# Row factors of four norms from a spread sum: inverse root on ScalarE and one Newton step, beside re-pinned copies and transposes

## Chip, cores and metric

The kernel runs on one core of a Trainium2 chip. The metric is the device time in microseconds of one execution. PE is TensorE, DVE is VectorE, ACT is ScalarE, POOL is GpSimd, SP is SyncE (which issues most DMAs). PSUM is the memory that matmuls write to, SBUF the one that the other engines work in.

## The reference

One layer of a hybrid encoder, S = 512 tokens, D = 2048 channels, float32:

```python
xn   = rms_norm(x, attn_norm_g)                    # norm 1, over 2048 channels
proj = xn @ w_in                                   # u_val, u_gate, q, k, v: 1024 columns each
h    = u_val * sigmoid(u_gate)                     # group A
h    = depthwise_conv(h, 31 taps) + dw_b
y_a  = silu(layer_norm(h, ln_g, ln_b))             # norm "ln", over 1024 channels
y_b  = neighborhood_attention(q, k, v, rpb)        # group B: 16 heads of 64, window 8 x 16 on an 8 x 64 grid
mixed = concat(rms_norm(y_a, conv_out_g), rms_norm(y_b, na_out_g))   # norms "a" and "na"
x    = x + mixed @ w_out
up   = depthwise_conv(rms_norm(x, ffn_norm_g) @ w_up, 3 taps) + b    # norm 2; 2 x 5632 columns
x    = x + (silu(gate) * val) @ w_down
out  = rms_norm(x, final_norm_g)                   # norm 3
```

Each norm needs, for every token, one over the root of (mean square + 1e-6).

## The kernel before

Activations lie with channels on the 128 partitions and tokens along the free axis, so a factor per token has to be known on all partitions: a tile of 128x512 whose rows are all alike. Products are made in parts: every float32 operand is split in a high and a low float32r tile, and one product becomes three matmuls (`mm3`, L124 to L129: high by high L127, high by low L128, low by high L129). The weights arrive in units of 128x1024 (`raw`, DMA by SP); `parts` (L113 to L118) has ACT copy the high half (`whi`, L116) and DVE subtract the low one (`wlo`, L117). Three units are prepared ahead of the one that PE reads, in four buffers.

The order of the work is written out: units follow a plan, and the first stage projects group A's columns (`a`), the values (`v`) and queries and keys (`q`) in the order "aavaav", four times "aq", "qqqq". After each weight unit `tick` advances two lists of generators, `steps` (norms, attention) and `asteps` (group A's tail), so that pieces of other work are placed between the products. `pin` (`tc.keep_in_program_order`) holds an instruction at its place in its engine's program order; the rest is ordered by a scheduler. Each engine executes its own queue in order.

The norms. `sum_sq` (L165 to L170) adds up squares over the 128-row pieces in a tile `acc`: ACT squares, DVE adds. What is left is a sum over partitions. `rsqrt_steps` (L179 to L214) makes it by one matmul of each 128 columns of `acc` with a column of ones (L190; 128x1, four of them for 512 tokens, each shown as two records in the trace), so that tokens lie on partitions; DVE and ACT make the root on 128x4 numbers (`root`, L172 to L177: Sqrt on ACT, reciprocal and a Newton step on DVE); DVE writes the factors into a diagonal matrix `dg`, high and low (L197, L201); two matmuls of ones with `dg` (L207) put them on all partitions, and ACT copies the result from PSUM (L213). It serves `rstd1` (norm 1), `rln` (ln), `ra` (a), `rna` (na), `rstd2` (norm 2) and `rstd3` (norm 3).

The places that the change touches:

- The start (L220 to L264): ACT makes `xh` with the gains `g1`, which DVE copies out of the first load (L263).
- `project_v` (L310 to L338): the first half's products (`pv`, L324 to L326) end in four PSUM banks. ACT copies each, scaled by the tokens' factor, to `vg` (L335) and `vx` (L338). Three of the banks are the three that `project` cycles through.
- `group_a` (L389 to L418): the mean (`yh`, `yl`, `st` L396, `mu` L398), differences (L401), the factor `rln`, then y·rln (L410), the swish, the splits `ma`, the sums of squares and the factor `ra`.
- The attention turns table and scores by 128x128 transposes on PE (`trp`, L503), 16 for a group.
- `norm_b` (L590) makes `rna`, `stats2` (L662 to L671) makes `rstd2` from two sums that come back by DMA.
- The tail (L991 to L1059). Tokens 0 to 383 are finished with channels on partitions: `finish` (L975 to L989) multiplies by gain and factor, for pairs 0, 2, 3, 5 and 6 on DVE (`fin`, L985, factor `st` read in PSUM), for pairs 1, 4 and 7 on POOL (L983, factor `rb`, a copy in SBUF that ACT makes at L1015). The last 128 tokens are turned and multiplied meanwhile (`pt`, L1028 to L1035); their own factor comes from row sums by ACT (L1038), a root (L1047 to L1051), and the results leave as `out_N` (L1059) behind the `out_T` of `finish`, all on SP's queue.

Of the kernel before, what the change touches and what calls it, by code (L numbers as in the profile page):

```python
# [16 lines left out]
P = 128  # L17
# [49 lines left out]
def layer(ctx: ExitStack, tc: tile.TileContext, xT, xG, xw, w_a, w_in, w_v, w_out, w_up, w_down, par, tab, g3, out, last_out):  # L67
# [23 lines left out]

    pin = tc.keep_in_program_order

    g1 = consts.tile([P, KD], F32, name="g1")
# [18 lines left out]
    def parts(raw, n):  # L113
        hi = wpool.tile([P, U * P], F32R, tag="whi", name="whi", bufs=NW)
        lo = wpool.tile([P, U * P], F32R, tag="wlo", name="wlo", bufs=NW)
        i = nc.scalar.activation(hi[:, :n], raw[:, :n], AF.Copy)  # L116
        j = nc.vector.tensor_sub(lo[:, :n], raw[:, :n], hi[:, :n].bitcast(F32))  # L117
        return hi, lo, i, j  # L118
# [5 lines left out]
    def mm3(ps, w, wk, mh, ml, start, stop):  # L124
        hi, lo = w[:2]
        a = slice(wk * P, (wk + 1) * P)
        nc.tensor.matmul(ps, hi[:, a], mh, start=start, stop=False)  # L127
        nc.tensor.matmul(ps, hi[:, a], ml, start=False, stop=False)  # L128
        return nc.tensor.matmul(ps, lo[:, a], mh, start=False, stop=stop)  # L129


    steps, asteps = [], []
# [31 lines left out]
    def sum_sq(acc, src, first, to=slice(0, S)):  # L164
        if first:  # L165
            nc.scalar.activation(acc, src, AF.Square)
        else:
            q = t2("sq")[:, to]
            nc.scalar.activation(q, src, AF.Square)
            nc.vector.tensor_add(acc, acc, q)  # L170

    def root(r, y, v):  # L172
# [6 lines left out]
    def rsqrt_steps(acc, n, name, to=slice(0, S), keep=True, by_token=None, free=False, rest=1, hold=False):  # L179

        def bank():
            if free:
                return psa.tile([P, 2, S], F32, tag="sc", name="st")[:, 0]
            return psa.tile([P, S], F32, tag="po", name="st")

        m = (to.stop - to.start) // P
        ps = bank()[:, :m]
        v, r, y = (sm.tile([P, S // P], F32, tag="rs" + c, name="rs" + c)[:, :m] for c in "vry")
        for i in range(m):
            nc.tensor.matmul(ps[:, i:i + 1], acc[:, to.start + i * P:to.start + (i + 1) * P], ones[:, 0:1],  # L190
                             start=True, stop=True)
        nc.vector.tensor_scalar(v, ps, 1.0 / n, EPS, op0=ALU.mult, op1=ALU.add)
        root(r, y, v)
        if by_token is not None:
            by_token.append(y)
        ds = [t2("dg", F32R)[:, :m * P] for _ in range(2)]
# [6 lines left out]
        for _ in range(rest):  # L203
            yield
        ps = bank()[:, :m * P]
        for i, dg in enumerate(ds):
            m = nc.tensor.matmul(ps, ones_r, dg, start=i == 0, stop=i == 1)  # L207
            if hold:
                pin(m)
        if not keep:  # L210
            return ps
        res = t2(name)
        nc.scalar.activation(res, ps, AF.Copy)  # L213
        return res  # L214
# [18 lines left out]
    for k in range(KD):  # L233
# [28 lines left out]
        if k == 0:  # L262
            pin(nc.vector.tensor_copy(g1, raw[:, n - KD:n]))  # L263
    with tc.issue_after(last.ins):  # L264
# [18 lines left out]
    def stats1():  # L283
        yield
        for k in range(CH, KD):
            with tc.issue_after(made[0][3].ins):
                sum_sq(acc1, x1[k], False)
            if k % 4 == 3:
                yield
        for _ in range(STAT_AT):  # L290
            yield
        rstd.append((yield from rsqrt_steps(acc1, D, "rstd1", by_token=rtok)))

    steps.append(stats1())

    def project(n):
        ps = psm.tile([P, S], F32, tag="mm", name="pj")
        for u in range(KD // U):
            w = weights()
            for k in range(U):  # L300
                kk = u * U + k
                m = mm3(ps, w, k, xs[kk][0], xs[kk][1], kk == 0, kk == KD - 1)
            tick(m)
            while late and rstd:
                late.pop(0)()
        return ps
# [3 lines left out]
    def project_v(half):  # L310
# [22 lines left out]
        with shifted(-600):  # L333
            for t, ps in enumerate(banks):
                nc.scalar.activation(vg[half][t], ps, AF.Copy, scale=y[:, t:t + 1])  # L335
                for x, rows in ((t - 1, slice(0, DH)), (t, slice(DH, P))):
                    if 0 <= x < len(vx[half]):
                        nc.scalar.activation(vx[half][x][rows], ps[rows], AF.Copy, scale=y[rows, t:t + 1])  # L338

# [49 lines left out]
    def group_a():  # L389
        h, l = t2("yh", F32R), t2("yl", F32R)  # L390
        nc.scalar.activation(h, ysum[0], AF.Copy)
        nc.vector.tensor_sub(l, ysum[0], h.bitcast(F32))
        yield
        ps = psa.tile([P, S], F32, tag="po", name="st")
# [5 lines left out]
        for i in range(NC_):  # L400
            nc.vector.tensor_sub(ys[i], ys[i], mu)  # L401
# [93 lines left out]
    def turn(ts):  # L495
        pts, first = {}, True
        for n in (2, 3, 0, 1):
# [31 lines left out]
    def attention():  # L529
# [18 lines left out]
        values(*before)  # L548
        yield

# [39 lines left out]
    def norm_b():  # L590
        r = yield from rsqrt_steps(acc_na, NA, "rna")
        for i in range(NP_):
# [69 lines left out]
    def stats2():  # L662
# [5 lines left out]
        nc.vector.tensor_add(acc2, acc2, q)  # L668
# [323 lines left out]
    for d in range(KD):  # L992
        ps = psm.tile([P, S], F32, tag="mm", name="pd")[:, fm]
        for k in range(n):
            mm3(ps, ws[d // CH * CH + k], d % CH, hs[k][0][:, fm], hs[k][1][:, fm], k == 0, k == n - 1)
        nc.vector.tensor_add(x2[d][:, fm], x2[d][:, fm], ps)
# [4 lines left out]
    stats, rb, xg = rsqrt_steps(acc, D, "rstd3", to=fm, keep=False, hold=True), [], []  # L1001
# [4 lines left out]
    def spread(g, k):  # L1006
        if (g, k) == (0, 1):
            next(stats)
        elif (g, k) == (1, 2):
            try:  # L1010
                next(stats)
            except StopIteration as e:
                rb.append(e.value)
            rb.append(t2("rb")[:, fm])
            nc.scalar.activation(rb[1], rb[0], AF.Copy)  # L1015
        for at in pairs[:2 if rb else 0]:
            pairs.remove(at)
            finish(at, rb[at % 3 == 1], at % 3 == 1, at % 3 != 1)

    for g, ps in enumerate(banks):  # L1020
# [5 lines left out]
        for k in range(n):  # L1026
            (hh, hl), (dh, dl) = hs[k], ws[g * CH + k]
            i = nc.tensor.matmul(ps, hh[:, tm], dh, start=False, stop=False)  # L1028
            if (g, k) == (1, 2):
                pin(i)  # L1030
                spread(g, k)
            i = nc.tensor.matmul(ps, hl[:, tm], dh, start=False, stop=False)
            if (g, k) == (1, 2):
                pin(i)
            nc.tensor.matmul(ps, hh[:, tm], dl, start=False, stop=k == n - 1)  # L1035
            if (g, k) != (1, 2):
                spread(g, k)
        nc.scalar.activation(t2("sq"), ps, AF.Square, accum_out=sums[:, g:g + 1])  # L1038
# [10 lines left out]
    nc.vector.reciprocal(r, r)  # L1049
    nc.vector.scalar_tensor_tensor(y, r, w, r, op0=ALU.mult, op1=ALU.mult)  # L1050
# [86 lines left out]
```

## Time and profile before

| | us |
|---|---|
| median of three runs | 2025.43 (2024.95, 2025.43, 2026.96) |
| profiled execution, its own time | 2026.78 |
| its span in the profile | 2025.0 |
| PE busy | 2013.7 (99%) |
| DVE busy | 1668.0 (82%) |
| ACT busy | 1052.0 (52%) |
| POOL busy | 168.7 (8%) |

The profile shows one execution. In a line of its timeline stand the start, the duration, the engine, the line of the kernel, the operation, what it writes and reads, the shapes and, with x, how many stand together; in brackets the idle time of the engine just before it and what ended it. A line of the waits names the waiting group, what it waited for, and the sum, count and largest wait. A line of the windows gives length, busy time and count for PE, PEld (TensorE's loading of weights), DVE, ACT and POOL, the clock granted to TensorE (1 is full), the share of the DMA engines and the GB/s that they moved. Matmuls overlap in PE's pipeline, so the distance between two starts, not the duration, is what one costs.

### The profile page before, as it was taken

How to read it: one execution, taken by the hardware profiler on the slowest of the kernel's cores; microseconds unless marked ns; L12 is line 12 of the kernel's file. 1: busy time of each engine (PE TensorE's matmuls, PEld its weight loads, DVE VectorE, ACT ScalarE, POOL GpSimd, SP SyncE). 2: the span in 40 equal slices, each digit the busy share in tenths (PEclk: the TensorE clock that was granted, in tenths of full speed). 3: DMA queues.
4: the chain of work that ended last, by engine and by line, in shares of the span. 5: the costliest groups of instructions: out<-in, count | busy, mean ns of one | idle time of the engine just before them, and what ended most of it. 6: DMA issues, size and time to landing. Idle time of an engine off the chain costs nothing.

```text
span 2025.0 us, 28150 instructions
## 1 busy us (share of the span) xinstructions
PE 2013.7 (99%) x10556; PEld 1721.0 (85%) x10556; DVE 1668.0 (82%) x2300; ACT 1052.0 (52%) x1686; POOL 168.7 (8%) x199
## 2 busy tenths in 40 slices
PE   9999999999999999999999999999999999999998
PEld 8788888888888998888888888888888888888887
DVE  7976888988577899888888888888888888879875
ACT  6323344466346555555555555555555555555563
POOL 0000000000001101111111111111111111110111
PEclk9999999999999999999999999999999999999999
DMA  7223333336338765565565565565565565564573
GB/s 257 94 85 93 113 94 106 106 112 231 104 119 214 198 167 146 125 146 146 125 146 146 129 142 146 127 143 146 118 153 146 125 146 146 125 144 127 146 201 132
DMA packets 98935, 284.25 MB, mean 140 GB/s; under 512 B 10992, under 2 KB 12272, under 8 KB 98800
## 3 DMA queue, kind: packets, MB, share of 16 engines
q1 hardware_dynamic: 72144, 231.07, 36.8%
q0 software_dynamic: 26656, 51.39, 16.9%
q8 instruction: 83, 1.36, 0.3%
q14 instruction: 52, 0.43, 0.1%
HBM read 227.89 MB, written 54.53 MB: 139 GB/s over the span
## 4 chain that ended last, share of the span: by engine, by line
PE 98%; DVE 1%; ACT 0%; issue 0%; DMA 0%; ACTq 0%; DVEq 0%
PE pu L759 27%; PE pu L765 14%; PE pd L129 8%; PE pd L127 8%; PE pd L128 8%; PE pj L127 6%; PE pj L129 5%; PE pj L128 5%; PE po L127 3%; PE po L129 3%; PE po L128 3%; PE pv L325 1%; PE pv L324 1%; PE pv L326 1%; PE trp L503 1%; PE pu L127 1%
## 5 line engine op out<-in xcount | busy, mean ns | idle before, releaser
L116 ACT ACTIVATE whi<-raw 128x1024 fp32r<-128x1024 f32 x364 | 384.6, 1058 | 507.8 <-PE pj L128 137.9
L117 DVE TENSOR_TENSOR wlo<-raw,whi 128x1024 fp32r<-128x1024 f32 x364 | 444.4, 1222 | 210.1 <-ACT whi L116 203.3
L759 PE MATMUL pu<-xc,whi 128*128 128x512 f32 x2352 | 580.0, 391 | 0.0
L759 PEld LDWEIGHTS pu<-xc,whi 128*128 128x128 f32 x2352 | 433.5, 188 | 83.0
L765 PEld LDWEIGHTS pu<-xc,wlo 128*128 128x128 f32 x2352 | 306.9, 191 | 14.7
L765 PE MATMUL pu<-xc,wlo 128*128 128x256 f32 x2352 | 311.4, 282 | 0.0
L129 PE MATMUL pd<-hh,wlo 128*128 128x512 f32 x640 | 250.3, 391 | 0.0
L127 PE MATMUL pd<-hh,whi 128*128 128x512 f32 x640 | 249.7, 390 | 0.0
L128 PE MATMUL pd<-hl,whi 128*128 128x512 f32 x640 | 249.1, 389 | 0.0
L913 POOL DMA_DIRECT2D x2d<-pdc x160 | 139.4, 873 | 1097.8 <-ACT pdc L912 870.9
L127 PE MATMUL pj<-xh,whi 128*128 128x512 f32 x512 | 199.6, 394 | 2.3 <-ACT vx L338 2.2
L129 PE MATMUL pj<-xh,wlo 128*128 128x512 f32 x512 | 199.2, 392 | 0.0
L128 PE MATMUL pj<-xl,whi 128*128 128x512 f32 x512 | 198.9, 391 | 0.0
L791 ACT ACTIVATE pl<-pu 128x256 f32<-128x256 f32 x294 | 109.8, 382 | 149.9 <-PE pu L759 142.8
L379 DVE SCALAR_TENSOR_TENSOR y<-ch,prm,y 128x500 f32<-128x500 f32 (+14 forms) x240 | 173.5, 740 | 4.3
L116 ACT ACTIVATE whi<-ws 128x1024 fp32r<-128x1024 f32 x132 | 139.7, 1058 | 70.9 <-PE pu L759 55.2
L117 DVE TENSOR_TENSOR wlo<-ws,whi 128x1024 fp32r<-128x1024 f32 x132 | 161.1, 1221 | 14.8 <-ACT whi L116 14.8
L129 PEld LDWEIGHTS pd<-hh,wlo 128*128 128x128 f32 x640 | 120.1, 188 | 28.5 <-DVE wlo L117 3.3
L128 PEld LDWEIGHTS pd<-hl,whi 128*128 128x128 f32 x640 | 120.2, 188 | 24.9 <-DVE hl L898 0.3
L127 PEld LDWEIGHTS pd<-hh,whi 128*128 128x128 f32 x640 | 120.4, 188 | 22.6
L912 ACT ACTIVATE pdc<-pd 128x512 f32<-128x512 f32 x160 | 93.8, 588 | 79.3 <-PE pd L129 66.2
L127 PEld LDWEIGHTS pj<-xh,whi 128*128 128x128 f32 x512 | 96.6, 189 | 23.5 <-ACT vx L338 2.6
(220 smaller groups left out, 2728.9 us busy)
## 6 DMA issues: line engine op xcount, KB each, us to landing
raw<-in_w_up SPq DMA_DIRECT2D x176, 512.0 KB, 3.8
raw<-in_w_down SPq DMA_DIRECT2D x88, 512.0 KB, 4.0
x2d<-pdc POOLq DMA_DIRECT2D x160, 256.0 KB, 4.9
raw<-in_w_in SPq DMA_DIRECT2D x60, 512.0 KB, 3.8
raw<-in_w_out SPq DMA_DIRECT2D x32, 512.0 KB, 3.7
raw<-in_w_v SPq DMA_DIRECT2D x16, 512.0 KB, 3.7
tab<-in_tab SPq DMA_DIRECT2D x32, 256.0 KB, 5.1
x<-in_xT SPq DMA_DIRECT2D x16, 256.0 KB, 5.4
```

Source lines behind the costliest of these rows:

```text
L116: i = nc.scalar.activation(hi[:, :n], raw[:, :n], AF.Copy)
L117: j = nc.vector.tensor_sub(lo[:, :n], raw[:, :n], hi[:, :n].bitcast(F32))
L127: nc.tensor.matmul(ps, hi[:, a], mh, start=start, stop=False)
L128: nc.tensor.matmul(ps, hi[:, a], ml, start=False, stop=False)
L129: return nc.tensor.matmul(ps, lo[:, a], mh, start=False, stop=stop)
L324: nc.tensor.matmul(ps, xh, wh[:, f], start=kk == 0, stop=False)
L379: nc.vector.scalar_tensor_tensor(y[:, a:b], h[:, a + j - PAD:b + j - PAD], prm[:, o + j:o + j + 1], y[:, a:b], op0=ALU.mult, op1=ALU.add)
L759: i = nc.tensor.matmul(ps, w[0][:, k * P:(k + 1) * P], comb[c][k], start=k == 0, stop=stop and k == ks[-1])
L765: i = nc.tensor.matmul(ps[:, H:], w[1][:, k * P:(k + 1) * P], comb[c][k][:, :H], start=False, stop=stop and k == U - 1)
L791: nc.scalar.activation(to, ps, AF.Copy)
L912: nc.scalar.activation(t, ps, AF.Copy)
L913: nc.gpsimd.dma_start(xd[d], t, accum_op=ALU.add)
```

## The change

It has six parts.

- Four norms (`rln`, `ra`, `rna`, `rstd2`) and `rstd3` no longer sum into columns. In the new `spread`, ACT copies `acc` to a high part `nh` and DVE makes the low part `nl`; two matmuls with a 128x128 matrix of ones put the sum over the partitions on every partition at once; ACT applies the inverse root straight to PSUM (scale 1/n, bias eps), and three DVE instructions of full width make a Newton step. `factor` wraps it. `rstd1` keeps the old way (`factor_and_tokens`), since its factors are needed by token too; its root uses the same inverse root instead of Sqrt and reciprocal.
- `project_v` pins its copies in order, and the next `whi` copy is pinned behind them (`copied`).
- The first product behind a group of transposes is pinned (`turned`).
- `tick` can advance `asteps` once in the middle of a unit; `group_a`'s mean uses it. The numbers of steps between parts of the norms are set anew.
- The copy of `g1` at the start moves from DVE to ACT.
- In the tail one `rstd` in SBUF serves DVE and POOL, the products with `nh` and `nl` stand at another place of the loop, a dummy inverse root on ACT stands in the middle of the last channel loop, and the last tokens' root is an inverse root, without the reciprocal.

```diff
@@ parts
         i = nc.scalar.activation(hi[:, :n], raw[:, :n], AF.Copy)
+        if copied:
+            copied.pop()
+            pin(i)
@@ mm3
-        nc.tensor.matmul(ps, hi[:, a], mh, start=start, stop=False)
+        m = nc.tensor.matmul(ps, hi[:, a], mh, start=start, stop=False)
+        if turned:
+            turned.pop()
+            pin(m)
@@ tick
-    def tick(behind):
+    def tick(behind, mid=False):
         for todo in (steps, asteps):
-            while todo:
+            while todo and mid == (todo is asteps and amid[0]):
                 try:
                     with tc.issue_after(behind.ins):
-                        next(todo[0])
+                        at = next(todo[0])
+                    if todo is asteps:
+                        amid[0] = at == "mid"
                     break
@@ root
-        nc.scalar.activation(r, v, AF.Sqrt)
-        nc.vector.reciprocal(r, r)
+        nc.scalar.activation(r, v, AF.Abs_reciprocal_sqrt)
@@ in place of rsqrt_steps (whose old body stays for rstd1 as factor_and_tokens)
+    def spread(acc, to, n, name, bank, hold=False):
+        m = to.stop - to.start
+        h, l = (t2("n" + c, F32R)[:, :m] for c in "hl")
+        nc.scalar.activation(h, acc[:, to], AF.Copy)
+        nc.vector.tensor_sub(l, acc[:, to], h.bitcast(F32))
+        yield
+        ps = bank()[:, :m]
+        for i, x in enumerate((h, l)):
+            x = nc.tensor.matmul(ps, ones_r, x, start=i == 0, stop=i == 1)
+            if hold:
+                pin(x)
+        r, q = t2(name)[:, :m], t2("q")[:, :m]
+        nc.scalar.activation(r, ps, AF.Abs_reciprocal_sqrt, scale=1.0 / n, bias=eps)
+        nc.vector.scalar_tensor_tensor(q, r, -0.5 / n, r, op0=ALU.mult, op1=ALU.mult)
+        nc.vector.scalar_tensor_tensor(q, ps, n * EPS, q, op0=ALU.add, op1=ALU.mult)
+        nc.vector.scalar_tensor_tensor(r, q, 1.5, r, op0=ALU.add, op1=ALU.mult)
+        return r
...
+    def factor(acc, n, name, rest=1, free=False):
+        steps = spread(acc, slice(0, S), n, name, lambda: stat_bank(free))
+        next(steps)
+        for _ in range(rest):
+            yield
...
@@ the start
-            pin(nc.vector.tensor_copy(g1, raw[:, n - KD:n]))
+            pin(nc.scalar.activation(g1, raw[:, n - KD:n], AF.Copy))
@@ project
                 m = mm3(ps, w, k, xs[kk][0], xs[kk][1], kk == 0, kk == KD - 1)
+                if k == U // 2:
+                    tick(m, mid=True)
@@ project_v
-                nc.scalar.activation(vg[half][t], ps, AF.Copy, scale=y[:, t:t + 1])
+                pin(nc.scalar.activation(vg[half][t], ps, AF.Copy, scale=y[:, t:t + 1]))
...
-                        nc.scalar.activation(vx[half][x][rows], ps[rows], AF.Copy, scale=y[rows, t:t + 1])
+                        pin(nc.scalar.activation(vx[half][x][rows], ps[rows], AF.Copy, scale=y[rows, t:t + 1]))
+        copied.append(half)
@@ group_a
-        yield
+        yield "mid"
...
-        yield
-        yield
-        r = yield from rsqrt_steps(acc, CONV, "rln")
+        r = yield from factor(acc, CONV, "rln", rest=3)
+        yield
...
-        yield
-        yield
-        ra.append((yield from rsqrt_steps(acc, CONV, "ra")))
+        ra.append((yield from factor(acc, CONV, "ra", rest=2)))
@@ attention
+        turned.append(pts)
         return pts
...
         values(*before)
-        yield
@@ norm_b, stats2
-        r = yield from rsqrt_steps(acc_na, NA, "rna")
+        r = yield from factor(acc_na, NA, "rna")
...
-        yield
-        yield
-        rstd2.append((yield from rsqrt_steps(acc2, D, "rstd2", free=True, rest=5, hold=True)))
+        rstd2.append((yield from factor(acc2, D, "rstd2", rest=2, free=True)))
@@ the tail
+        if d == KD // 2:
+            with tc.issue_after(i.ins):
+                pin(nc.scalar.activation(idle, eps, AF.Abs_reciprocal_sqrt))
...
+    rows = spread(acc, fm, D, "rstd3", stat_bank, hold=True)
+    next(rows)
...
-            rb.append(t2("rb")[:, fm])
-            nc.scalar.activation(rb[1], rb[0], AF.Copy)
...
-            finish(at, rb[at % 3 == 1], at % 3 == 1, at % 3 != 1)
+            finish(at, rb[0], at % 3 == 1, at % 3 != 1)
...
-    nc.scalar.activation(r, v, AF.Sqrt)
+    nc.scalar.activation(r, v, AF.Abs_reciprocal_sqrt)
     nc.vector.tensor_scalar(w, v, -0.5, None, op0=ALU.mult)
-    nc.vector.reciprocal(r, r)
```

More of the change, by code (lines that the diff above doesn't have):

```diff
@@ new lines, in stat_bank, with factor_and_tokens @@
+    def stat_bank(free=False):
+        if free:
+            return psa.tile([P, 2, S], F32, tag="sc", name="st")[:, 0]
+        return psa.tile([P, S], F32, tag="po", name="st")
+    def factor(acc, n, name, rest=1, free=False):
[3 more added lines that the diff above has]
+            yield
+        try:
+            next(steps)
+        except StopIteration as e:
+            return e.value
+    def factor_and_tokens(acc, n, name, by_token):
+        m = S // P
+        ps = stat_bank()[:, :m]
+        v, r, y = (sm.tile([P, m], F32, tag="rs" + c, name="rs" + c) for c in "vry")
@@ L189, in rsqrt_steps @@
         for i in range(m):
-            nc.tensor.matmul(ps[:, i:i + 1], acc[:, to.start + i * P:to.start + (i + 1) * P], ones[:, 0:1],
-                             start=True, stop=True)
+            nc.tensor.matmul(ps[:, i:i + 1], acc[:, i * P:(i + 1) * P], ones[:, 0:1], start=True, stop=True)
         nc.vector.tensor_scalar(v, ps, 1.0 / n, EPS, op0=ALU.mult, op1=ALU.add)
         root(r, y, v)
-        if by_token is not None:
-            by_token.append(y)
-        ds = [t2("dg", F32R)[:, :m * P] for _ in range(2)]
+        by_token.append(y)
@@ L197, in rsqrt_steps @@
+        ds = [t2("dg", F32R) for _ in range(2)]
         nc.vector.tensor_mul(ds[0].rearrange("p (i k) -> p i k", k=P), ident.unsqueeze(1).broadcast_to([P, m, P]),
@@ L202, in rsqrt_steps @@
                                            op0=ALU.mult, op1=ALU.subtract)
-        for _ in range(rest):
-            yield
-        ps = bank()[:, :m * P]
+        yield
+        ps = stat_bank()
         for i, dg in enumerate(ds):
[L207 to L211, printed above, removed]
+            nc.tensor.matmul(ps, ones_r, dg, start=i == 0, stop=i == 1)
         res = t2(name)
@@ L291, in stats1 @@
             yield
-        rstd.append((yield from rsqrt_steps(acc1, D, "rstd1", by_token=rtok)))
+        rstd.append((yield from factor_and_tokens(acc1, D, "rstd1", rtok)))
     steps.append(stats1())
```

34 lines of the change are left out of this document (14 added, 20 removed).

## The prediction

> **What bounds the kernel now.** I read the page first: span, engines, chain.
>
> ```profile
> span 2025.0 us, 28150 instructions
> PE 2013.7 (99%) x10556; PEld 1721.0 (85%) x10556; DVE 1668.0 (82%) x2300; ACT 1052.0 (52%) x1686; POOL 168.7 (8%) x199
> PE 98%; DVE 1%; ACT 0%; issue 0%; DMA 0%; ACTq 0%; DVEq 0%
> ```
>
> TensorE (PE) is busy 2013.7 of 2025.0 us and carries 98% of the chain that ended last, so a microsecond counts if PE loses or saves it, or if it lies in the tail behind the last product. DVE (82%) costs nothing by itself, except where PE waits for its result. Then I read the waits of PE for the longest one, and the timeline and the windows around it:
>
> ```profile
> PE pj L127 <- ACT vx L338: 2.2, 1, 2.2
> 94.15 0.39 PE L326 MATMUL pv<-wlo,xh 128*128 128x512 f32 x1
> 94.35 1.06 ACT L116 ACTIVATE whi<-raw 128x1024 fp32r<-128x1024 f32 x1 [4.38 <-PE pv L325]
> 95.32 0.67 ACT L335 ACTIVATE vg<-pv,rsy 128x512 f32<-128x512 f32 x1
> 96.00 0.68 ACT L338 ACTIVATE vx<-pv,rsy 64x512 f32<-64x512 f32 x1
> 96.73 0.50 PE L127 MATMUL pj<-xh,whi 128*128 128x512 f32 x1 [2.19 <-ACT vx L338]
> 97.70:101.20 3.50, 3.50 (x10) 2.69 (x10) 3.39 (x6) 3.44 (x6) 0.00 (x0) 0.51 0.49 145
> ```
>
> After the first value projection PE needs the first of three banks back. ACT has idled 4.38 us, then makes a whi of a later unit before it copies vg and vx out of that bank, and PE stands. The last line (length; busy PE, PEld, DVE, ACT, POOL with counts; granted clock; DMA share; GB/s) has PE at half clock for 3.5 us right behind it. These are the only microseconds which PE loses in one piece.
>
> **The change, part by part.** All sums are first against the profiled execution: 2026.78 us, of which the span is 2025.0. The median of the three runs shown is 2025.43, 1.35 lower.
>
> *A, the bank's release.* The pins put that whi behind the copies. Bank 0's last product starts nine steps of 0.23 (rows in B) before 94.15, at 92.1, and ends at 92.5, so vg and vx (0.67 + 0.68) are done about 93.9, before PE is there at 94.38. The stall of 96.73 − 94.38 = 2.35 (94.38 is the step after 94.15) goes. The whi, moved to the end of the copies at about 99.4, belongs to a unit that PE reads about 110; that hides it, and without that cover it would cost its own 1.06. The half clock cost 3.50 × (1 − 0.51) = 1.71. Gone with its cause: A = −2.35 − 1.71 = −4.06. Whether every execution loses that clock, one trace can't say; against the median I credit half, so +0.85 there. By the Trainium skill (page "TensorE: Matmul & The Clock Gate", section "What's actually happening") the clock falls only after an idle window of about 3.4 us; the trace disagrees, 2.35 us of rest stand ahead of the 0.51. By that rule A would be −2.35 and the sum 1.71 higher.
>
> *B, the sums over columns.* Four norms lose eight 128x1 products each; the two products with dg become two with nh and nl, at no cost.
>
> ```profile
> L190 PE MATMUL st<-ones,acc x38: 164/250/271, 41.5 to 2006.1; 128*128 128x1 f32 x38
> 433.39 0.39 PE L129 MATMUL pj<-xh,wlo 128*128 128x512 f32 x1
> 434.90 0.49 PE L127 MATMUL pj<-xh,whi 128*128 128x512 f32 x1
> 561.16 0.39 PE L129 MATMUL po<-mah,wlo 128*128 128x512 f32 x1
> 561.39 0.95 PE L190 MATMUL st<-ones,accna 128*128 128x1 f32 x8
> 562.20 0.49 PE L127 MATMUL po<-mah,whi 128*128 128x512 f32 x1
> 562.52 0.40 PE L128 MATMUL po<-mal,whi 128*128 128x512 f32 x1
> 562.75 0.40 PE L129 MATMUL po<-mah,wlo 128*128 128x512 f32 x1
> ```
>
> At the na norm the product before the columns starts at 561.16, the third behind them at 562.75: 1.59, where three steps of 0.23 (562.52 to 562.75) take 0.69. So eight columns cost 0.90. At rln the gap is 434.90 − 433.39 = 1.51 against 562.20 − 561.16 = 1.04, so 0.90 + 0.47 = 1.37 (a wait for acc is in it). The first row (38 alike, rstd1's eight stay) lets me take 0.90 for ra and 0.90 for rstd2. B = −4.07. On the other engines, a diagonal on DVE becomes one copy on ACT, one subtraction and three 512-wide steps on DVE, 0.6 to 0.7 each; they cost where PE waits (E, F).
>
> *C, transposes.* Six groups split 12 + 4 become 16 in a row.
>
> ```profile
> 442.73 0.40 PE L129 MATMUL pj<-xh,wlo 128*128 128x512 f32 x1
> 443.03 0.66 PE L503 MATMUL trp<-ident,tab 128*128 128x128 f32 x4
> 443.44 0.48 PE L127 MATMUL pj<-xh,whi 128*128 128x512 f32 x1
> 443.76 0.39 PE L128 MATMUL pj<-xl,whi 128*128 128x512 f32 x1
> ```
>
> Entering takes 0.30 and the product after leaving 0.32 where 0.23 is the step: 0.07 + 0.09, about 0.14 with rounding. C = 6 × 0.14 = −0.84, between 0 and −1.
>
> *D, the start.* ACT makes the g1 copy it now waits for.
>
> ```profile
> 5.79 0.72 ACT L251 ACTIVATE xh<-raw,g 128x512 fp32r<-128x512 f32 x1 [1.31 <-DVE g L263]
> ```
>
> At most the 1.31 goes, at least nothing, if another input is late next; I take −0.3.
>
> *E, ra's norm.* In the changed kernel's order on PE the two products with nh and nl stand right behind twelve transposes, some 6 us of PE work earlier than the pair they replace. PE is in order; whatever is late there stops everything queued behind, the last ma products and four transposes first.
>
> ```profile
> 413.74 0.69 DVE L398 TENSOR_SCALAR mu<-st 128x512 f32<-128x512 f32 x1 [2.95 <-PE st L396]
> 414.35 1.22 DVE L117 TENSOR_TENSOR wlo<-raw,whi 128x1024 fp32r<-128x1024 f32 x1
> 415.48 2.49 DVE L401 TENSOR_TENSOR y<-y,mu 128x512 f32<-128x512 f32 x4
> 444.85 1.90 DVE L410 TENSOR_TENSOR y<-y,rln 128x512 f32<-128x512 f32 x3 [2.07 <-ACT rln L213]
> 473.81 1.47 PE L503 MATMUL trp<-ident,tab 128*128 128x128 f32 x12
> 477.28 0.69 DVE L170 TENSOR_TENSOR acc<-acc,sq 128x512 f32<-128x512 f32 x1
> ```
>
> The sum for mu is moved four products up, so mu starts at 413.74 − 0.91 = 412.83. Between mu and the first y·rln DVE has 37 instructions at 0.60 (2.49 for four) and four wlo at 1.13 (414.35 to 415.48), with hops some 27.4: y·rln at about 440.3, 4.5 earlier. From there to the end of the last acc takes, as before, 477.97 − 444.85 = 33.1: 473.4. A wlo stands ahead of nl (1.13), then nl 0.69: 475.2. PE is there at 473.81 − 1.37 − 0.14 + 1.23 (twelve transposes) + 0.23 = 473.8. So a new PE wait of 1.4 us; bounds 0 and 4 (ACT's and DVE's order may slip by two wlo). Half a clock window behind it, up to 1.71, stays in the range.
>
> *F, rstd2.* No eight columns, but nh and nl, with another engine step between, now follow an add that a DMA releases:
>
> ```profile
> 683.66 0.69 DVE L668 TENSOR_TENSOR acc<-acc,sq 128x512 f32<-128x512 f32 x1 [0.57 <-DMA sq<-sq]
> ```
>
> nh ends about 685.0 and nl about 686.1; PE comes to them about 686.0 and 686.2. I take +0.2, between 0 and 1.5.
>
> Without the tail: −4.06 − 4.07 − 0.84 − 0.3 + 1.4 + 0.2 = −7.67.
>
> *G, the tail.*
>
> ```profile
> 2005.13 0.40 PE L1032 MATMUL pt<-dh,hl 128*128 128x512 f32 x1
> 2006.22 0.48 PE L1035 MATMUL pt<-dl,hh 128*128 128x512 f32 x1
> 2010.41 5.90 POOL L983 TENSOR_TENSOR fin<-x,rb 128x384 f32<-128x384 f32 x6 [37.65 <-ACT rb L1015]
> 2010.36 3.24 DVE L985 SCALAR_TENSOR_TENSOR fin<-x,prm,st 128x384 f32<-128x384 f32 x6 [0.47 <-ACT rb L1015]
> 2014.12 2.18 DVE L985 SCALAR_TENSOR_TENSOR fin<-x,prm,st 128x384 f32<-128x384 f32 x4
> 2015.44 2.50 SPq L987 DMA_DIRECT2D out_T<-fin  x4
> 2018.55 0.16 DVE L1049 RECIPROCAL rsr<-rsr 128x1 f32<-128x1 f32 x1
> 2019.71 1.82 SPq L1059 DMA_DIRECT2D out_N<-xg  x4
> ```
>
> The columns of rstd3 go (2006.22 − 2005.13 − 0.23 = 0.86) and the reciprocal (0.2): −1.1 if nothing else changes. But DVE's ten fin take their factor from st in PSUM today, while POOL's six take it from the copy rb in SBUF; they run side by side at 0.54 and 0.98 us. In the changed kernel both read x and one rstd in SBUF, at the same time, from about 2010.0. No row of before has DVE with two SBUF inputs beside POOL, so the cost lies between 0 and full turn-taking. If DVE's ten go first (5.4), POOL ends its fourth at 2010.0 + 5.4 + 3.9 = 2019.3; SP sends in order: that pair 0.45, four more 2.3 (2.50 now), the last pair 0.45, four out_N 1.82: 2024.3, against 2021.53 today, so about +2.7 for the tail. If they alternate, DVE's ten end near 2021.1 (5.4 + 5.9 later), and the second half of xg and the root behind them come 4.2 late. The Trainium skill speaks against this change here (page "SBUF — State Buffer", section "Who interferes with whom"): a DVE instruction with two SBUF inputs and a GpSimd instruction that reads SBUF exclude each other for a whole instruction; no run shown bears it out. I take +2.7, which lies between the bounds 0 − 1.1 and +4.2.
>
> Sum: −7.67 + 2.7 = −5.0: 2021.8 in the profiled execution's terms, 2025.43 − 5.0 + 0.85 = **2021.3** as a median.
>
> **The rivals.**
>
> No contention at the end: the two engines go on at 0.54 and 0.98. For it speaks that they overlap without loss today; against it, that DVE's second input moves from PSUM to where POOL reads. −7.67 − 1.1 = −8.8, so 2017.5.
>
> The new wait at ra is two to three us longer than I count, because ACT or DVE works off more of its queue ahead of nh and nl; 82% of DVE busy speaks for it. About 2024.
>
> It doesn't do what it says: something else still keeps the banks after project_v (say, the copies are released later than I read), the 2.35 and the clock remain: 2021.3 + 2.35 + 0.85 = 2024.5.
>
> Slower: the chain of group A on DVE doesn't move, because what set 444.85 was not the mean but the list between. Then the last acc ends at 477.97, nl about 479.8, and PE, waiting from 473.8, loses 6.0 instead of 1.4: +4.6, and two half-clock windows of 1.71 as behind the stall at 97 us: +3.4. 2021.3 + 8.0 = 2029.3. It gets slower than before once PE's wait at that place, clock included, exceeds my 1.4 by over 4.1.
>
> **How the numbers follow.** Tail contention as forecast 0.46 (own range 2020 to 2023.5: from half of it to alternating); no contention 0.26; the longer wait 0.11; no effect on the bank 0.06; slower 0.11. The range 2016.6 to 2024.6 takes the first four in, with about one microsecond below the no-contention sum for the clock that I credited half; it leaves out the slow case and the edges, under 2 in 10. A difference under 0.2% (4.05 us) can hardly be told from none here. Faster by over that is under 2021.38: all of no contention and half of the forecast, 0.49. Slower by over that is above 2029.48: half of the slow case, whose 2029.3 stands at that edge, 0.06. The rest, 0.45, is the same.
>
> **What the profile after would show.** A: no wait of PE on vx, granted clock 1.0 at 95 to 101 us, that whi behind nine copies. B: no 128x1 products but rstd1's. C: groups of 16 transposes. E: a PE wait on nl of 1 to 2 us behind twelve transposes near 470; none makes me wrong by 1.4, over 5 means the slow rival. G: mean durations of fin: if DVE's stay near 0.54 and POOL's near 0.98, I am wrong by 3.8 and the no-contention rival holds; if POOL's last fin ends some 5 us later than today relative to the last product, I am right. A loss spread evenly over PE's products, with the same waits, would make the whole way of counting wrong.

## The result: slower, not faster

The changed kernel takes 2031.95 us (median of nine runs, 2030.62 to 2032.47), the kernel before 2026.67 in the same nine rounds: a ratio of 1.0029, 95% interval [1.0019, 1.0038]. The forecast was 2021.3, with 2024.6 as the upper end. In the profiled executions it is 2031.56 against 2026.78, +4.78 us.

The kernel before has two levels, and its medians lie on one or the other by chance: 24 runs of one later comparison stand at 2024.92 to 2025.88 (11) and at 2026.63 to 2027.77 (13), about 1.6 apart. The traced execution, one of the upper level, has the half clock behind the stall on vx; run 6, without that stall, has one level alone.

The head of the page, the chain and the waits of PE, after:

```profile
span 2029.8 us, 28055 instructions
PE 2008.3 (99%) x10518; PEld 1715.8 (85%) x10518; DVE 1672.3 (82%) x2269; ACT 1052.8 (52%) x1688; POOL 170.5 (8%) x199
PE 97%; DVE 1%; ACT 1%; DMA 0%; issue 0%; ACTq 0%; DVEq 0%
PE trp L537 <- ACT pt L542: 6.2, 6, 1.1
PE po L131 <- DVE oa L637: 2.4, 2, 2.0
```

PE is busy for 5.4 us less than before, and yet the span is 4.8 longer. The wait on vx is gone; six waits of 0.85 to 1.07 on a copy of a turned tile (`pt`, in six of the eight groups; two groups stay split) and two on `oa` have come. To see how much each place is worth, I take the same instruction in both traces and subtract its starts; what the difference changes by between two such marks was won or lost there:

| mark (before, after) | difference | change, and what lies in the stretch |
|---|---|---|
| first product of pv (50.86, 51.22) | +0.36 | +0.36, the start |
| last product of pv (184.86, 181.10) | −3.76 | −4.12, project_v |
| last value product of the attention (555.61, 556.45) | +0.84 | +4.60, rln, ra and the transposes |
| first product with mbh (584.58, 587.47) | +2.89 | +2.05, rna |
| last product pu (1947.71, 1949.62) | +1.91 | −0.98, rstd2 |
| end of the span (2025.0, 2029.8) | +4.8 | +2.9, the tail |

**project_v.** ACT's timeline and the window of the half clock, after:

```profile
92.90 0.69 ACT L371 ACTIVATE vg<-pv,rsy 128x512 f32<-128x512 f32 x1 [2.56 <-PE pv L362]
93.60 0.68 ACT L374 ACTIVATE vx<-pv,rsy 64x512 f32<-64x512 f32 x1
...
99.41 2.00 ACT L117 ACTIVATE whi<-raw 128x1024 fp32r<-128x1024 f32 x2
97.70:101.20 3.50, 3.50 (x17) 2.92 (x16) 3.36 (x6) 3.49 (x5) 0.00 (x0) 1.00 0.00 0
```

vg starts at 92.90 instead of 95.32, the whi follows at 99.41, and the clock is 1.00 with 17 products where 10 had fitted.

**The transposes.** The timeline around the first group, before and then after:

```profile
258.11 1.48 PE L503 MATMUL trp<-ident,tab 128*128 128x128 f32 x12
259.04 1.56 ACT L508 ACTIVATE pt<-trp 128x512 f32<-128x512 f32 x3
260.65 0.66 PE L503 MATMUL trp<-ident,tab 128*128 128x128 f32 x4
```

```profile
254.34 1.47 PE L537 MATMUL trp<-ident,tab 128*128 128x128 f32 x12
255.27 1.55 ACT L542 ACTIVATE pt<-trp 128x512 f32<-128x512 f32 x3
256.88 0.66 PE L537 MATMUL trp<-ident,tab 128*128 128x128 f32 x4 [1.07 <-ACT pt L542]
```

In both, the thirteenth transpose starts right after ACT's third copy (260.60 and 256.82). Before, five products filled the time between (from 259.34; the expectation of run 1 says six). The pin took them away, and PE stands.

**The na norm.** Rows of DVE, and the product that waits, after:

```profile
560.06 0.69 DVE L637 TENSOR_TENSOR oa<-po,ra 128x512 f32<-128x512 f32 x1
565.29 0.69 DVE L205 SCALAR_TENSOR_TENSOR q<-rna 128x512 f32<-128x512 f32 x1 [0.78 <-ACT rna L204]
567.47 1.90 DVE L627 TENSOR_TENSOR ao<-ao,rna 128x512 f32<-128x512 f32 x3
575.00 0.69 DVE L637 TENSOR_TENSOR oa<-po,ra 128x512 f32<-128x512 f32 x1
575.75 0.50 PE L131 MATMUL po<-mah,whi 128*128 128x512 f32 x1 [1.99 <-DVE oa L637]
```

Between two oa, each of which frees a bank of PSUM, DVE has the Newton step (565.29 to 567.47) and the products and splits of the norm. Before, the next oa came at 566.56 and 577.52, eleven microseconds apart; here it is fifteen.

**The tail.** The fin, and SP's last output, after:

```profile
2011.80 9.91 DVE L1017 SCALAR_TENSOR_TENSOR fin<-x,prm,rstd 128x384 f32<-128x384 f32 x10
2011.91 7.80 POOL L1015 TENSOR_TENSOR fin<-x,rstd 128x384 f32<-128x384 f32 x6 [37.23 <-DVE rstd L207]
2021.63 0.68 DVE L1077 TENSOR_TENSOR xg<-pt,g3b 128x512 f32<-128x512 f32 x1
2022.16 0.41 SPq L1021 DMA_DIRECT2D out_T<-fin  x1
2024.56 1.80 SPq L1091 DMA_DIRECT2D out_N<-xg  x4
```

Ten fin on DVE take 9.91 instead of 5.4, six on POOL 7.80 instead of 5.90, and xg, which leads to the last tokens' root, stands behind them. SP has issued the last out_T at 2022.57 and then waits for that root until 2024.56; meanwhile the DMA engines run nearly empty. The groups of fin by line (shortest, median and longest duration in ns), and a window of that pause:

```profile
L1017 DVE SCALAR_TENSOR_TENSOR fin<-x,prm,rstd x10: 605/1350/1374, 2011.8 to 2021.1; 128x384 f32<-128x384 f32 x10
L1015 POOL TENSOR_TENSOR fin<-x,rstd x6: 1308/1321/1385, 2011.9 to 2018.4; 128x384 f32<-128x384 f32 x6
2024.20:2025.20 1.00, 0.00 (x0) 0.00 (x0) 0.99 (x2) 1.00 (x2) 0.00 (x0) 0.50 0.17 65
```

The two engines take turns. While POOL works, DVE's fin start 1.27 to 1.30 us apart (2012.34, 2013.63, 2014.93 and so on), one to each fin of POOL; the three that start after POOL has ended are 0.53 apart.

### The profile page after: what moved, and what is told of

The parts are those of the page before. It is cut to its first block, busy times and chain, and to the rows that moved or that the text cites. A ratio compares the mean times of both kernels' runs of the same rounds, so it can differ in the third digit from the quotient of the medians.

```text
span 2029.8 us, 28055 instructions
## 1 busy us (share of the span) xinstructions
PE 2008.3 (99%) x10518; PEld 1715.8 (85%) x10518; DVE 1672.3 (82%) x2269; ACT 1052.8 (52%) x1688; POOL 170.5 (8%) x199
## 4 chain that ended last, share of the span: by engine, by line
PE 97%; DVE 1%; ACT 1%; DMA 0%; issue 0%; ACTq 0%; DVEq 0%
PE pu L791 26%; PE pu L797 14%; PE pd L136 8%; PE pd L131 8%; PE pd L135 8%; PE pj L131 6%; PE pj L135 6%; PE pj L136 6%; PE po L131 3%; PE po L135 3%; PE po L136 3%; PE pv L361 1%; PE pv L360 1%; PE pv L362 1%; PE po L553 1%; PE pu L135 1%
```

## The experiments

All stand against before in the same rounds; to compare with the changed kernel I use its median, 2031.95. The two levels of before are the same in all the rounds (2024.9 to 2025.9 and 2026.5 to 2027.8).

**1. The group of transposes without the pin.**

```diff
-        turned.append(pts)
         return pts
```

> The changed kernel without the pin that puts the next product behind a group of transposes. Theory T: the new 6.2 us of PE waiting on the copy of a turned tile come from that pin alone, which took six products out from between the twelfth and the thirteenth transpose; without it the groups stand as 12 + 4 again, the wait on pt is 0, and the time falls by 6.5 to 7.2 us to about 2025. Since those waits also gave DVE slack ahead of the ra norm, up to 1.4 us of waiting on nl near 470 us may come back, then 2026 to 2026.5. Rival R: ACT is late there in any case, the six waits move to the split place or to the next user of the banks; less than 2 us gained.

Measured: 2025.38 us (ratio to before 0.9997, [0.9988, 1.0006]), 6.6 less than with the pin. The groups stand as 12 + 4, and no wait on pt is left. So the pin alone cost those waits. From the end of project_v to the attention's last value product this run takes 2.09 us less than before (−4.32 at the one mark, −6.41 at the other), the changed kernel 4.60 more: the pin cost 6.69. The wait on nl did not come.

**2. The pin kept, the copy issued later.**

```diff
-        pts, first = {}, True
+        pts, first, held = {}, True, []
...
-            pts[n] = t2("pt").rearrange("p (c k) -> p c k", c=4)
-            nc.scalar.activation(pts[n], ps, AF.Copy)
+            held.append((n, ps))
+            while held and n:
+                x, src = held.pop(0)
+                pts[x] = t2("pt").rearrange("p (c k) -> p c k", c=4)
+                nc.scalar.activation(pts[x], src, AF.Copy)
```

> The changed kernel with the pin kept, but in each group the copy of the third turned tile is issued behind the transposes of the fourth, which shares a two-bank tile with it. Theory T: the thirteenth transpose waits for that copy only because both halves are one tile; with the copy behind it the group is 16 in a row without a wait, and besides the 6.9 us some 0.8 us of switching saved in comparison with 12 + 4: about 2024.5 to 2025. Rival R: the wait is for a bank that ACT truly has to empty (the first two copies, or ACT's queue); then 1 us of wait for each group stays and the time is within 1 us of the changed kernel's.

Measured: 2023.95 us (0.9991, [0.9982, 0.9999]), 8.0 less than the changed kernel. The timeline of the first group:

```profile
254.05 1.91 PE L537 MATMUL trp<-ident,tab 128*128 128x128 f32 x16
254.99 2.10 ACT L545 ACTIVATE pt<-trp 128x512 f32<-128x512 f32 x4
```

Sixteen in 1.91 us without a wait, though ACT copies no sooner: the third and fourth turned tile are halves of one tile of two banks, and a transpose into the second half waited for the copy that reads the first, as long as that copy was issued ahead of it. Sixteen in a row are also worth about what I had worked out for them: from the end of project_v to the attention's last value product this run takes 3.29 us less than before, the one without the pin 2.09. All eight groups are 16 in a row here, so each is worth 0.15.

**3. The na norm one unit later.**

```diff
-        r = yield from factor(acc_na, NA, "rna")
+        r = yield from factor(acc_na, NA, "rna", rest=2)
```

> The changed kernel with the products of the na norm one weight unit later, as far behind their inputs as the diagonal's products stood before. Theory T: the 2.4 us of PE waiting on oa near 573 and 581 us arise because the factor is ready a unit earlier, so DVE's list of eight products and splits starts ahead of the oa that frees a bank; with one oa ahead of it again the wait is gone, -2.0 to -2.7 us, about 2029.5. Rival R: DVE has simply more to do there (three full-width Newton steps against a few 128x4 ones), the wait stays or moves to the splits that the second half of the output projection reads, and nothing is gained or something lost.

Measured: 2031.5 us (1.0027, [1.0016, 1.0038]), a gain of 0.45 that nothing separates from none. Theory T fell: an oa does go ahead (561.83), but the wait is still there, 2.4 us in two, since the next one comes at 579.85. The rival's first half was right: DVE has more to do in one piece there. From the first Newton step to the oa behind the list it takes 9.7 us, as in the changed kernel (565.29 to 575.00), where before the list began with the first ao at 569.99 and its oa followed 7.5 later; the 2.2 in between are three Newton steps of 0.72.

**4. The last factor in PSUM for DVE.**

```diff
...
-        nc.vector.scalar_tensor_tensor(r, q, 1.5, r, op0=ALU.add, op1=ALU.mult)
+        o = ps if both else r
+        nc.vector.scalar_tensor_tensor(o, q, 1.5, r, op0=ALU.add, op1=ALU.mult)
+        return o
...
-    rows = spread(acc, fm, D, "rstd3", stat_bank, hold=True)
+    rows = spread(acc, fm, D, "rstd3", stat_bank, hold=True, both=True)
...
+            rb.append(t2("rb")[:, fm])
+            nc.scalar.activation(rb[1], rb[0], AF.Copy)
...
-            finish(at, rb[0], at % 3 == 1, at % 3 != 1)
+            finish(at, rb[at % 3 == 1], at % 3 == 1, at % 3 != 1)
```

> The changed kernel with the last Newton step of the final norm written to PSUM for DVE, and an ACT copy in SBUF for POOL, as before the change. Theory T: DVE's ten fin took 0.99 us and POOL's six 1.30 because both read two operands from SBUF at the same time; DVE returns to 0.54 and POOL to 0.98 each, the end comes 3.5 to 4.5 us earlier: about 2027.5 to 2028.5. Rival R: what slows them is something else in the tail (the output DMAs, the later place of the factor); the fin stay near 1.0 and the time within 1 us.

Measured: 2029.2 us (1.0016, [1.0007, 1.0025]), 2.75 less than the changed kernel; the least gain of 3.5 that I gave was too high. The groups of fin (in such a line stand the group's busy time and the mean ns of one, which overlaps the next):

```profile
L1018 DVE SCALAR_TENSOR_TENSOR fin<-x,prm,st 128x384 f32<-128x384 f32 x10 | 5.3, 608 | 0.6 <-ACT rb L1051 0.6
L1016 POOL TENSOR_TENSOR fin<-x,rb 128x384 f32<-128x384 f32 x6 | 5.9, 1011 | 38.1 <-ACT rb L1051 38.1
```

Both are as before the change. From the last pu product to the end this tail is as long as before's (the difference to before is +2.42 at the one and +2.4 at the other), although the columns are off PE. What took their gain is asked in the last experiment.

**5. A copy of the factor for POOL alone.**

```diff
+            rb.append(t2("rb")[:, fm])
+            nc.scalar.activation(rb[1], rb[0], AF.Copy)
...
-            finish(at, rb[0], at % 3 == 1, at % 3 != 1)
+            finish(at, rb[at % 3 == 1], at % 3 == 1, at % 3 != 1)
```

> The changed kernel with a second SBUF copy of the final factor, made by ACT, for POOL's six fin; DVE's ten still read x and their factor from SBUF. Theory T: the price comes from DVE reading two operands in SBUF while POOL reads two, not from sharing one tile; then DVE's fin stay near 1.0 us and POOL's near 1.3 while both run, and the time stays within 1 us of the changed kernel's 2032. Rival R: the two engines collide on the one factor tile; then DVE returns to 0.54, POOL to 0.98, and the time to 2028.5 to 2029.5 as with the factor in PSUM.

Measured: 2031.99 us (1.003, [1.002, 1.0041]), as the changed kernel.

```profile
L1017 DVE SCALAR_TENSOR_TENSOR fin<-x,prm,rstd 128x384 f32<-128x384 f32 x10 | 9.9, 1060 | 0.0
L1015 POOL TENSOR_TENSOR fin<-x,rb 128x384 f32<-128x384 f32 x6 | 7.8, 1334 | 36.2 <-ACT rb L1050 36.2
```

It isn't the shared factor tile: with two tiles both engines are as slow.

**6. Before, with the pins of project_v alone.**

```diff
+    copied = []
...
+        if copied:
+            copied.pop()
+            pin(i)
...
-                nc.scalar.activation(vg[half][t], ps, AF.Copy, scale=y[:, t:t + 1])
+                pin(nc.scalar.activation(vg[half][t], ps, AF.Copy, scale=y[:, t:t + 1]))
...
-                        nc.scalar.activation(vx[half][x][rows], ps[rows], AF.Copy, scale=y[rows, t:t + 1])
+                        pin(nc.scalar.activation(vx[half][x][rows], ps[rows], AF.Copy, scale=y[rows, t:t + 1]))
+        copied.append(half)
```

> The kernel before with only the pinned copies of project_v and the next whi pinned behind them. Theory T: the wait of 2.35 us on vx goes, and with it the half clock behind it wherever an execution had it: the time falls by 2.35 to 4.1 us against before, the clock is full between 95 and 102 us. Rival R: the half clock has another cause and stays, or the moved whi makes the next product late; less than 2.3 us gained.

Measured: 2022.66 us (2022.44 to 2022.87; 0.9983, [0.9974, 0.9992]). The two levels of before have become one, 2.5 us under the median of the lower and 4.1 under that of the upper. That fits the stall of 2.35 in every execution and the half clock of 1.71 in those of the upper level; the trace has full clock there.

**7. oa ahead of the tick's work.**

```diff
-            tick(i)
-            read(d, ps)
+            early = m is ma and ra
+            if early:
+                read(d, ps)
+            tick(i)
+            if not early:
+                read(d, ps)
```

> The changed kernel with the products of the na norm where the change has them, but in the first half of the output projection the oa and x that free a bank are issued ahead of the other work of a tick instead of behind it. Theory T (after the run with the norm one unit later, which kept its wait): three Newton steps of 0.72 us now stand on DVE between the na factor and eight products and splits, in one uninterrupted list of 9.7 us instead of 7.5, and the oa behind that list frees its bank too late; ahead of the list, it takes the wait of 2.0 to 2.4 us away: about 2029.5. Rival R: the list then ends 1.3 us later and the second half of the projection waits for mbh and mbl instead, less than 1 us gained.

Measured: 2028.36 us (1.0011, [1.0002, 1.002]), 3.6 less than the changed kernel. No wait on oa is left (one oa now starts at 562.26, ahead of the Newton step), and from the attention to the first mbh product the stretch is 0.94 shorter than before: what the eight columns had cost. The gain is larger than the waits of the changed kernel's profile (2.4), for two reasons. Each stop costs PE more than its idle time: by the marks the stretch is 2.99 shorter than in the changed kernel (−0.94 against +2.05). And the waits bring the half clock in some executions. Run 1, which has one wait of 2.0 us there, shows it in the window behind that wait,

```profile
565.15:568.56 3.41, 1.42 (x8) 0.84 (x6) 3.41 (x7) 2.50 (x4) 0.00 (x0) 1.00 0.00 0
568.56:571.97 3.41, 3.41 (x8) 2.74 (x9) 3.41 (x5) 0.77 (x2) 0.00 (x0) 0.50 0.00 0
```

(clock 0.50), and the changed kernel's own profile does not. In the four traces with that half clock the stretch is 2.94 to 2.97 longer than before, so 3.9 longer than here; the gain of 3.6 in the medians lies between 2.99 and 3.9.

**8. Three edits together (2, 4 and 7).**

> The changed kernel with three of the edits together: the copy of the third turned tile behind the transposes of the fourth, the factor in PSUM for DVE with a copy for POOL, and oa ahead of the tick's other work. Theory T: the three losses are separate, so their gains add up: 8.0 + 2.8 + 2.2 from 2032, about 2019, which is 6.4 us under before. Rival R: taking the waits away on PE only makes the last norm or the projection late in another place, as the slack of DVE that they gave is gone: 2021 to 2024.

Measured: 2017.75 us (2017.67 to 2018.28), ratio 0.996, [0.9947, 0.9974]: faster than both kernels, by 8.9 us against before's median in that comparison and 14.2 against the changed kernel. The gains add up (8.0, 2.75 and 3.6 alone, 14.35 in sum), as theory T has it; about 2019 was forecast because the third was put at 2.2. PE's only wait left is that of its warm-up at the start. At the last pu product it stands 9.53 us ahead of before; the tail loses 0.3 again (9.3 ahead at the end).

**9. All sixteen fin on DVE.**

```diff
-            finish(at, rb[0], at % 3 == 1, at % 3 != 1)
+            finish(at, rb[0], False, at % 3 != 1)
```

> The changed kernel with all sixteen fin on DVE, both operands in SBUF as in the change, and none on POOL. Theory T: two operands in SBUF are slow only beside POOL; alone DVE takes 0.53 to 0.56 us for each, sixteen in 8.6 us instead of ten in 9.9, and the time falls by 1 to 2 us against the changed kernel's 2032. Rival R: DVE reads two SBUF operands more slowly in itself; then each takes about 1.0, sixteen take 16 us and the time rises by 5 us or more.

Measured: 2030.54 us (1.0024, [1.0014, 1.0034]), 1.4 less than the changed kernel.

```profile
L1017 DVE SCALAR_TENSOR_TENSOR fin<-x,prm,rstd 128x384 f32<-128x384 f32 x16 | 8.6, 609 | 0.0
```

Sixteen alone take less than ten beside POOL, 0.54 each. Two operands in SBUF are not slow for DVE; they are slow while POOL reads its own two.

**10. The factor sooner (8 without the last norm's Newton step).**

```diff
+        if both:
+            nc.vector.tensor_copy(ps, r)
+            return ps
         nc.vector.scalar_tensor_tensor(q, r, -0.5 / n, r, op0=ALU.mult, op1=ALU.mult)
```

> The kernel with three edits mended, less the Newton step of the final norm (a copy to PSUM in place of three steps; the step's refinement is left out), so that the factor is known 1.2 us sooner. Theory T: taking the columns off PE did not shorten the tail because the end follows from the moment at which the factor is known, over 4.2 MB of output that keep the DMA queues full; the time falls by 0.8 to 1.2 us, until the last tokens' own root, 0.6 us before the first out_N, becomes the limit. Rival R: the last products on PE and what follows them set the end; the time stays within 0.3 us of 2017.75.

Measured: 2016.74 us (0.9956, [0.9943, 0.997]), 1.0 less than in 8, as theory T has it. SP's last lines and a window of the last stretch, of 8 and then of this one:

```profile
2008.63 0.41 SPq L1029 DMA_DIRECT2D out_T<-fin  x1
2009.14 2.85 SPq L1101 DMA_DIRECT2D out_N<-xg  x4
2008.00:2012.00 4.00, 0.00 (x0) 0.00 (x0) 1.54 (x5) 1.40 (x3) 0.00 (x0) 0.61 1.02 380
```

```profile
2007.73 0.45 SPq L1032 DMA_DIRECT2D out_T<-fin  x1
2009.37 1.82 SPq L1104 DMA_DIRECT2D out_N<-xg  x4
2008.00:2012.00 4.00, 0.00 (x0) 0.00 (x0) 1.79 (x6) 1.54 (x3) 0.00 (x0) 0.82 1.02 378
```

In both, and before the change, the DMA engines are busy all the time there (share 1.01 to 1.02, 376 to 380 GB/s), so the end follows from when the output begins. From the last pu product to the first out_T it takes 63.3 us before and 63.4 in 4 and 8: the new chain to the factor, with its three full-width Newton steps, is as long as the old one with its columns. Here it takes 62.2, and the end comes 1.0 sooner. The out_N now wait 1.2 us for the last tokens' root; how much a still earlier factor would bring is not shown.

## Why the prediction was wrong, step by step

Two steps failed, both at places where PE waits for nothing before the change: the bounds of C, and in B the sentence that the longer work on DVE costs where PE waits, at E and F.

- **A** (−4.06): right. −4.12 in the profile, 2.5 to 4.1 by run 6. The half clock credited against the median was a hedge: a median of two levels lies on one of them, on the upper one in the nine rounds of the result.
- **B** (−4.07): right for the work, wrong for one norm. rstd2 gave −0.98 and rna −0.94 once its wait was gone (−0.90 each was forecast), rln and ra together −2.09 (run 1, with its transposes as before; −2.27 was forecast). But the change itself had +2.05 at rna. The step that failed is "they cost where PE waits (E, F)": I looked for late results at ra and rstd2 only, and there at what the factor itself releases. At rna it is the oa queued behind the list, and the 2.2 us of Newton steps ahead of it. Error: +2.95.
- **C** (−0.84): the largest error. In the changed kernel +6.69 (4.60, less the −2.09 of rln and ra), 7.5 worse than forecast. The size of the saving was right (0.15 a group, run 2 against run 1; 0.14 was forecast, though its two terms add up to 0.16), but the step "between 0 and −1" failed: these bounds left out that the split had hidden something. The row was there to be read: the thirteenth transpose started 0.05 us behind the end of ACT's third copy, which five products just covered. I priced what entering and leaving cost and never asked what those products were waiting through.
- **D** (−0.3): nothing shown. xh starts 0.50 sooner (5.29 instead of 5.79), but it then waits for a DMA, and the first pv product lies between −0.27 and +0.36 of before's in the ten traces with the changed start.
- **E** (+1.4): not put to the test as forecast. In the changed kernel the two products do stand right behind the twelve transposes, nl ends at 474.62 and PE takes it at 474.68, 0.1 late; but PE had stood 4.0 us in four of the new waits by then. In runs 1, 2 and 8, which have none of them, the two products stand some 7 us behind the first of the transposes (run 8: 467.53 and 475.02), and nl has been done for 4 us (470.86). Brought back by the 4.31 that run 8 was ahead after project_v, that is 475.2, the forecast time of nl; with PE where it was forecast, at 473.8, there would have been the wait, and that is in no trace. The slower rival at this place, and that of a longer wait, did not come.
- **F** (+0.2): no wait there in any trace.
- **G** (+2.7 for the tail): right in kind; that the size is nearly right, +2.9, is luck. The cause is shown by run 9 against the changed kernel and by run 4, and run 5 excludes the shared tile. But 2.7 came from the case that DVE's ten go first and SP's order behind POOL's last pair sets the end, and its sign was POOL's last fin some 5 us later relative to the last product. It is 1.5 later relative to the last pd product, and DVE's last 3.5. What came is the other case, the two in turns, with xg and the root late: +4.2 by my count, with 0.98 + 0.53 = 1.51 for a pair of fin. A pair took 1.29, and six times 0.22 less is 1.3: 2.9. By the Trainium skill (page "SBUF — State Buffer", section "Who interferes with whom") a DVE instruction with two SBUF inputs contends with a GpSimd instruction that reads SBUF, and the lock is exclusive. The trace agrees in the turns, one to one; 0.22 us of a pair still overlaps. The gain of 1.1 that I gave the case without contention is not there (run 4): the columns lay beside the chain to the factor, and that chain, with the output behind it, ends the tail (run 10).

The sum now: +0.36 − 4.12 − 2.09 + 6.69 + 2.05 − 0.98 + 2.9 = +4.8, the difference of the spans. Had C and rna gone as forecast, it would have been −5.7, close to the −5.0 that was forecast. Neither was among my rivals. My slower case looked for one large wait on the new chain; it was the small regular wait that the old order had covered, six times.

What stays open: at rna a shorter list on DVE (the Newton step elsewhere) was not tried as a cure beside the oa ahead of the list, and rln and ra were not measured apart from each other.

## What to carry to other kernels

Before merging a split group on an engine that does not wait, look at what the piece between covers: if the next member starts within a tenth of a microsecond of another engine's end, the filler may be hiding a wait, and the dependency (here a copy issued ahead of a write to the other half of its tile) has to go first. When a factor's arithmetic changes from a few small numbers to full width, count the time it adds to the list it now heads, and find what was queued behind that list. In the tail, ask which chain the end hangs on before crediting work taken off the busiest engine.

## What the runs showed of the hardware

DVE with two operands in SBUF took 0.54 us for 128x384 alone (run 9). Beside a POOL instruction that reads SBUF the two engines took turns, one instruction each in 1.29 us, where POOL's took 0.98 before the change; with one of DVE's operands in PSUM neither was slowed (run 4: 0.53 and 0.98).

A pause of 2.0 to 2.2 us on TensorE was followed by half clock in some executions and not in others of the same kind: before's 24 runs divide 13 to 11, and of the seven traces with the wait at rna four show it (runs 1, 4, 5 and 9) and three do not (the changed kernel, runs 2 and 3). The traces show what divides them. The half clock lasts 3.41 us each time, and the changes of the clock lie on a grid of that step: in before the fall at 97.75 and the one behind the last products at 2019.45 are 563 steps of 3.413 apart, in run 1 those at 568.56 and 2015.81 are 424. Where a trace has no half clock in between, the grid follows from the fall behind its last products. Windows on that grid, of before, then of run 2, each with the one that follows:

```profile
94.34:97.75 3.41, 1.22 (x5) 0.86 (x5) 3.41 (x5) 3.36 (x5) 0.00 (x0) 1.00 0.09 10
97.75:101.16 3.41, 3.41 (x9) 2.65 (x8) 3.30 (x6) 3.35 (x6) 0.00 (x0) 0.50 0.44 144
565.79:569.20 3.41, 1.63 (x7) 1.37 (x8) 3.41 (x6) 2.61 (x4) 0.00 (x0) 1.00 0.00 0
569.20:572.61 3.41, 3.41 (x17) 2.83 (x16) 3.41 (x5) 0.00 (x0) 0.00 (x0) 1.00 0.27 84
```

Where the whole pause lay in one window, PE was busy for 1.22 us of it (before) or 1.42 (runs 1, 4, 5 and 9), and half clock followed. Where it lay across two, the emptier of them had 1.63 (run 2), 1.71 (run 3) or 1.76 (the changed kernel), and the clock stayed full. So in these eight traces the limit is between 1.4 and 1.6 us of work in a window of 3.41; no run moved a pause on purpose to test it. If a pause of 2.19 us falls anywhere on the grid with equal chance, that limit takes the clock from 48 to 60% of the executions (an estimate); 13 of 24 is 54%. The Trainium skill (page "TensorE: Matmul & The Clock Gate", section "What's actually happening") gives an idle window of about 3.4 us as the condition; here a window that was idle for 1.99 us of its 3.41 was enough.
